# Two start-up loads of a hybrid decoder layer moved from SyncE's queue to ScalarE's

## The chip, the cores and the metric

One core of one Trainium2 chip runs the whole kernel. The metric is the device time of one execution in microseconds. A core has several engines with instruction streams of their own: TensorE (PE in the profile, with its weight loads as PEld), VectorE (DVE), ScalarE (ACT), GpSimd (POOL) and SyncE (SP). A DMA is issued by an instruction on one of them (SPq, ACTq, POOLq in the profile) and is then carried by the core's 16 DMA engines.

## The reference

One layer, float32, 512 tokens of width 1024:

```python
h = rms_norm(x, norm_mix_w)
proj = h @ w_in                       # z, xBC, dt, q, k, v, f
y_ssd = ssd_mixer(xbc, z, dt, ...)    # causal conv, SiLU, chunked scan, gated norm
y_fox = fox_mixer(q, k, v, f, ...)    # causal attention with forget gates
x = x + concat(y_ssd, y_fox) @ w_out
hf = rms_norm(x, norm_ffn_w)
x = x + conv_gated_mlp(hf, w_up, conv_w, conv_b, w_down)
```

## The kernel before

Every large product runs as three TensorE matmuls on split operands: each float32 operand is split into a high part (a rounding copy on ScalarE, names that end in `h`) and a low part (the rest, a subtraction on VectorE, names that end in `l`), and `mm3` (line 91) issues high x high, low x high and high x low. Weights come by `load_split` (lines 79 to 85) through three raw buffers.

The change is in the start-up. x arrives transposed in eight blocks of 128x512 (256 KB each, `load_x`, line 147), each into a buffer of its own. `split_x` turns block k into `xh[:, k]` on ScalarE (line 162) and `xl[:, k]` on VectorE (line 163), both scaled with a column of `mix`, the norm weights, which arrive in one tile with the small dt and forget-gate weights (`load_dt`, 132 KB: load at line 169, ScalarE's rounding at line 171, GpSimd's subtraction at line 172). The first feature tile's weights (tile 8 of xBC) arrive in two halves of 128x512 (256 KB, rows of 2 KB out of rows of 4 KB, `load_first`, line 153) and are split at lines 157 and 158. Half 0 holds the weights of x blocks 0 to 3, half 1 those of blocks 4 to 7. A 128x16 copy (line 113, `warm`) is ScalarE's first instruction, and the load of its activation table stands before it in the trace.

TensorE first multiplies a constant tile in 8 matmuls at line 188 that serve no output. Then for each block k it computes the dt and forget-gate columns (lines 196 and 200) and the first feature tile (`first_product`, line 91, three matmuls). For k = 0 only the dt matmuls run, with filler matmuls on the constant (line 184) between and after them; `first_product(0)` is put behind the dt matmuls of k = 1. The order around the first blocks is fixed in the program. The second feature tile (tile 10) follows on TensorE at once, its weights loaded and split by `load_split`.

All DMAs of the start-up are issued by SyncE, in this order: dt weights, x0, x1, first half of the feature weights, x2, x3, second half, x4 to x7, then constants, further weights and x in token order. An instruction list for each engine is fixed when the program is built, by a scheduler with a timeline of its own; engines run their lists in order. ScalarE's list in the start-up is: table load, warm copy, dt weights, x0, x1, first half, x2, x3, second half, x4 to x7.

Of the kernel before, what the change touches and what calls it, by code (L numbers as in the profile page):

```python
# [38 lines left out]
def tile_hybrid_layer(  # L39
# [20 lines left out]
    nc = tc.nc  # L60
    act, dve, pool, pe = nc.scalar, nc.vector, nc.gpsimd, nc.tensor
# [10 lines left out]
    def raw(ap):  # L72
        return ap.bitcast(F32)
# [36 lines left out]
    mhalf = cp.tile([P, 16], F32, tag="mhalf", name="mhalf")  # L110
    dve.memset(mhalf, -0.5)
    warm = cp.tile([P, 16], F32, tag="warm", name="warm")
    act.copy(warm, mhalf)

    x2 = cp.tile([P, NTB, D], F32, tag="x2", name="x2")

# [27 lines left out]

    def load_x(k):
        xr = px.tile([P, SEQ], F32, tag="xr", name="xr", bufs=NK)
        nc.sync.dma_start(xr, xT[k])
        return xr

    def load_first(half):  # L150
        c = slice(half * 512, (half + 1) * 512)
        w = px.tile([P, 512], F32, tag="wr", name="wr", bufs=2)
        nc.sync.dma_start(w, wxbc[8][:, c])
        return c, w

    def split_first(c, w):
        act.copy(first[0][:, c], w)
        dve.tensor_tensor(out=first[1][:, c], in0=w, in1=raw(first[0][:, c]), op=ALU.subtract)

    def split_x(k, xr):  # L160
        w = mix[:, k : k + 1]
        act.activation(xh[:, k, :], xr, AF.Copy, scale=w)
        dve.scalar_tensor_tensor(
            out=xl[:, k, :], in0=xr, scalar=w, in1=raw(xh[:, k, :]), op0=ALU.mult, op1=ALU.subtract
        )

    def load_dt():
        raw_dt = px.tile([P, NK + NK * 32], F32, tag="wdr", name="wdr")
        nc.sync.dma_start(raw_dt, wdtf)
        w = raw_dt[:, NK:].rearrange("p (k m) -> p k m", m=32)  # L170
        act.copy(wdt[:, :, 0:32], w)
        pool.tensor_tensor(out=wdt[:, :, 32:64], in0=w, in1=raw(wdt[:, :, 0:32]), op=ALU.subtract)
        return raw_dt[:, 0:NK]
# [12 lines left out]

    for _ in range(WARM):
        pe.matmul(spin[:, :P], ones, ones, start=True, stop=True)
    mix = load_dt()
    for k in range(NK):  # L190
        xr = load_x(k)
        split_x(k, xr)
        if k in (1, 3):
            split_first(*load_first(k // 2))
    for k in range(NK):
        ins = pe.matmul(pdt[:64, :], wdt[:, k, :], xh[:, k, :], start=k == 0, stop=False, skip_group_check=True)
        if k < 2:
# [504 lines left out]
    for half in range(2):  # L702
        c = slice(half * 512, (half + 1) * 512)
# [101 lines left out]
    def gated(j):  # L805
        both = []
        for part in range(2):
            f = part * NFF + j
            o = early[part] if j == 0 else up_proj((f,), 1)[0]
            xp = pu.tile([P, SEQ], F32, tag="up", name="up", bufs=3)  # L810
            dve.tensor_mul(xp, o, R2)  # L811
            a = pu.tile([P, SEQ], F32, tag="ua", name="ua", bufs=5)
            cw = C_FCW + 3 * f
            act.activation(a, xp, AF.Identity, scale=pc[:, cw + 2 : cw + 3], bias=pc[:, C_FCB + f : C_FCB + f + 1])
            for s in range(1, 3):
                dve.scalar_tensor_tensor(  # L816
                    out=a[:, s:], in0=xp[:, : SEQ - s], scalar=pc[:, cw + 2 - s : cw + 3 - s], in1=a[:, s:],
                    op0=ALU.mult, op1=ALU.add,
                )
            both.append(a)  # L820
        act.activation(both[0], both[0], AF.Silu)
        return both
# [12 lines left out]
    for j in range(NH):  # L835
# [5 lines left out]
        k, val = gated(j + NH)  # L841
# [178 lines left out]
```

## Time and profile before

| quantity | value |
|---|---|
| median of 3 runs | 799.24 us (798.89 to 799.96) |
| time of the profiled execution | 799.38 us |
| its span, first to last instruction | 797.6 us |
| TensorE busy | 790.3 us (99%) |
| VectorE, ScalarE, GpSimd busy | 567.6, 428.8, 224.4 us |
| mean granted TensorE clock | 0.999 of full speed |

Starts and durations are in us from the start of the span. A wait is attributed to what released it. "DMA to landing" is the time from the issue to the arrival of all data. The rows stand further below.

### The profile page before, as it was taken

What the parts mean: (1) busy time and instruction counts of PE and PEld (TensorE: products, weight loads), DVE (VectorE), ACT (ScalarE), POOL (GpSimd) and SP (SyncE); (2) the same over time, 40 slices, a digit from 0 to 9 for tenths busy, and PEclk for the clock granted to TensorE, in tenths of its full rate; (3) what the DMA queues carried; (4) which work ended last, traced back from release to release, by engine and by line L of the source; (5) the groups of instructions that cost most, each with busy time, mean ns of one, the idle gap of its engine ahead of it and who ended that gap; (6) DMA issues with size and microseconds to landing.
All of it is one profiled execution on the core that took longest, in us unless ns stands there. A gap on an engine that the chain in (4) does not pass through costs nothing.

```text
span 797.6 us, 10600 instructions
## 1 busy us (share of the span) xinstructions
PE 790.3 (99%) x3789; PEld 644.6 (81%) x3789; DVE 567.6 (71%) x889; ACT 428.8 (54%) x779; POOL 224.4 (28%) x260
## 2 busy tenths in 40 slices
PE   9999999999999999999999999999999999999997
PEld 6888878878887877887877888888888888888886
DVE  4896998688567575597874687676676676778754
ACT  7557556542478576776752554344344344556541
POOL 0004322433233352242101333223333223233120
PEclk9999999999999999999999999999999999999999
DMA  9514332341244244252221463323323323399982
GB/s 333 186 66 164 109 106 65 132 132 54 90 155 139 65 119 138 61 172 72 92 88 54 155 163 106 105 82 104 105 82 103 106 81 104 95 250 192 222 181 90
DMA packets 31253, 98.12 MB, mean 123 GB/s; under 512 B 3872, under 2 KB 4960, under 8 KB 31200
## 3 DMA queue, kind: packets, MB, share of 16 engines
q1 hardware_dynamic: 26192, 81.71, 31.0%
q0 software_dynamic: 4576, 15.21, 10.2%
q8 instruction: 30, 0.49, 0.3%
q10 hardware_dynamic: 432, 0.52, 0.2%
q14 instruction: 23, 0.19, 0.1%
HBM read 91.56 MB, written 2.20 MB: 118 GB/s over the span
## 4 chain that ended last, share of the span: by engine, by line
PE 98%; DMA 1%; SPq 0%; DVE 0%; ACT 0%; DVEq 0%; issue 0%
PE up L91 30%; PE pw L91 22%; PE po L91 11%; PE g L91 7%; PE Y L91 6%; PE X L91 4%; PE Z L91 4%; PE o L610 2%; PE pT L600 2%; PE yd L436 2%; PE j L91 1%; PE S L577 1%; PE S L578 1%; PE qkT L527 1%; PE yo L442 1%; PE st L449 1%
## 5 line engine op out<-in xcount | busy, mean ns | idle before, releaser
L84 ACT CAST wh<-wraw 128x1024 fp32r<-128x1024 f32 x103 | 108.0, 1049 | 109.6 <-PE up L91 75.2
L85 DVE TENSOR_TENSOR wl<-wraw,wh 128x1024 fp32r<-128x1024 f32 x103 | 132.8, 1289 | 26.2 <-ACT wh L84 23.9
L91 PE MATMUL up<-hh,wh 128*128 128x512 f32 (+1 forms) x360 | 138.9, 386 | 0.0
L91 PE MATMUL up<-hh,wl 128*128 128x512 f32 (+1 forms) x360 | 138.5, 385 | 0.0
L91 PE MATMUL up<-hl,wh 128*128 128x512 f32 (+1 forms) x360 | 138.5, 385 | 0.0
L91 PE MATMUL pw<-wh,xh 128*128 128x512 f32 x256 | 102.5, 402 | 0.0
L91 PE MATMUL pw<-wl,xh 128*128 128x512 f32 x256 | 101.8, 398 | 0.0
L91 PE MATMUL pw<-wh,xl 128*128 128x512 f32 x256 | 101.2, 397 | 0.0
L91 PEld LDWEIGHTS up<-hh,wh 128*128 128x128 f32 x360 | 67.6, 188 | 13.7 <-issue 0.2
L91 PEld LDWEIGHTS up<-hl,wh 128*128 128x128 f32 x360 | 67.7, 188 | 13.6 <-issue 0.2
L91 PEld LDWEIGHTS up<-hh,wl 128*128 128x128 f32 x360 | 67.6, 188 | 13.3
L811 DVE TENSOR_TENSOR up<-up,R 128x512 f32<-128x512 f32 x44 | 30.3, 691 | 58.5 <-PE up L91 58.5
L816 DVE SCALAR_TENSOR_TENSOR ua<-up,pc,ua 128x511 f32<-128x511 f32 (+1 forms) x88 | 66.8, 763 | 1.3
L91 PEld LDWEIGHTS pw<-wh,xl 128*128 128x128 f32 x256 | 48.2, 188 | 9.9 <-issue 0.5
L91 PEld LDWEIGHTS pw<-wl,xh 128*128 128x128 f32 x256 | 48.2, 188 | 9.6 <-issue 0.7
L91 PEld LDWEIGHTS pw<-wh,xh 128*128 128x128 f32 x256 | 48.1, 188 | 9.5 <-issue 0.7
L765 ACT CAST wh<-T 128x1024 fp32r<-128x1024 f32 (+1 forms) x30 | 29.3, 976 | 36.9 <-PE Z L91 15.3
L579 DVE CUSTOM_DVE_ANT_0 prob<-S,prob 128x128 f32<-128x128 f32 (+1 forms) x64 | 30.3, 487 | 24.7 <-PE S L578 24.4
L766 DVE TENSOR_TENSOR wl<-T,wh 128x1024 fp32r<-128x1024 f32 (+1 forms) x30 | 33.8, 1134 | 19.2 <-ACT wh L765 18.8
L583 ACT ACTIVATE prob<-prob,nm 128x128 f32<-128x128 f32 (+1 forms) x64 | 35.8, 560 | 21.1 <-DVE nm L579 20.4
L258 DVE TENSOR_TENSOR x<-po,x 128x512 f32<-128x512 f32 x48 | 32.6, 685 | 13.1 <-PE po L91 12.9
L826 POOL TENSOR_TENSOR ua<-ua 128x512 f32<-128x512 f32 x11 | 15.0, 1364 | 90.9 <-DVE ua L816 90.9
(231 smaller groups left out, 1690.0 us busy)
## 6 DMA issues: line engine op xcount, KB each, us to landing
wraw<-in_wup_dram SPq DMA_DIRECT2D x44, 512.0 KB, 3.3
T<-in_wdown_dram POOLq DMA_DIRECT2D x20, 512.0 KB, 6.9
wraw<-in_wqk_dram SPq DMA_DIRECT2D x16, 512.0 KB, 3.4
wraw<-in_wout_dram SPq DMA_DIRECT2D x16, 512.0 KB, 3.3
wraw<-in_wxbc_dram SPq DMA_DIRECT2D x11, 512.0 KB, 6.3
wraw<-in_wdown_dram SPq DMA_DIRECT2D x10, 512.0 KB, 3.5
T<-in_wdown_dram SPq DMA_DIRECT2D x10, 512.0 KB, 5.0
wraw<-in_wz_dram SPq DMA_DIRECT2D x8, 512.0 KB, 3.7
```

The costliest lines, as they stand in the source:

```text
L84: act.copy(h, r)
L85: dve.tensor_tensor(out=l, in0=r, in1=raw(h), op=ALU.subtract)
L91: ins = pe.matmul(o, a, b, start=start and n == 0, stop=stop and n == 2, **kw)
L258: dve.tensor_add(dst, banks[tb], dst)
L436: pe.matmul(yd[:, h * HD : (h + 1) * HD], sc[:, h, :], xdt[:, h * HD : (h + 1) * HD], start=True, stop=True)
L579: dve.tensor_tensor_reduce(out=p, in0=sps[:, :n], in1=p, scale=-1.0, scalar=-NEG, op0=ALU.add, op1=ALU.min, accum_out=nm[:, qb : qb + 1],)
L583: act.activation(p, p, AF.Exp, scale=-1.0, bias=nm[:, qb : qb + 1], accum_out=sm[:, qb : qb + 1])
L600: pe.transpose(t[:, w : w + P], prob[:, o : o + P], ident)
L765: act.copy(h[:, :n], src[:, :n])
L766: dve.tensor_tensor(out=l[:, :n], in0=src[:, :n], in1=raw(h[:, :n]), op=ALU.subtract)
L811: dve.tensor_mul(xp, o, R2)
L816: dve.scalar_tensor_tensor(out=a[:, s:], in0=xp[:, : SEQ - s], scalar=pc[:, cw + 2 - s : cw + 3 - s], in1=a[:, s:], op0=ALU.mult, op1=ALU.add,
```

## The change

The loads of x block 1 and of the first half of the feature weights are issued by ScalarE instead of SyncE, on ScalarE's own DMA queue, ahead of the warm copy. SyncE's list keeps the other loads in their old order, so it reads dt weights, x0, x2, x3, second half, x4 to x7. The splits keep their places in the program. No computation changes.

```diff
     warm = cp.tile([P, 16], F32, tag="warm", name="warm")
-    act.copy(warm, mhalf)
...
     def load_x(k):
         xr = px.tile([P, SEQ], F32, tag="xr", name="xr", bufs=NK)
-        nc.sync.dma_start(xr, xT[k])
+        (nc.scalar if k == 1 else nc.sync).dma_start(xr, xT[k])
         return xr
 
     def load_first(half):
         c = slice(half * 512, (half + 1) * 512)
         w = px.tile([P, 512], F32, tag="wr", name="wr", bufs=2)
-        nc.sync.dma_start(w, wxbc[8][:, c])
+        (nc.scalar if half == 0 else nc.sync).dma_start(w, wxbc[8][:, c])
         return c, w
...
     for _ in range(WARM):
         pe.matmul(spin[:, :P], ones, ones, start=True, stop=True)
+    xrs = {1: load_x(1)}
+    firsts = {0: load_first(0)}
+    act.copy(warm, mhalf)
     mix = load_dt()
     for k in range(NK):
-        xr = load_x(k)
-        split_x(k, xr)
+        split_x(k, xrs.pop(k, None) or load_x(k))
         if k in (1, 3):
-            split_first(*load_first(k // 2))
+            split_first(*(firsts.pop(k // 2, None) or load_first(k // 2)))
```

## Rows read from the trace of the kernel before

**Rows 1.** The page, busy time of TensorE over the whole span with its share and its number of matmuls and weight loads.

```profile
PE 790.3 (99%) x3789; PEld 644.6 (81%) x3789; DVE 567.6 (71%) x889; ACT 428.8 (54%) x779; POOL 224.4 (28%) x260
```

**Rows 2.** The view of waits for TensorE's matmuls, all of the span: who waited for whom, us in total, times, longest.

```profile
PE g L188 <- DVE mhalf L111: 1.0, 1, 1.0
PE g L91 <- ACT wh L157: 0.6, 1, 0.6
PE g L196 <- ACT xh L162: 0.3, 1, 0.3
```

**Rows 3.** The chain of work that ended last, in order of time, in the first 30 us: start, duration, what. The one piece that is a transfer.

```profile
2.11 4.64 DMA wr<-in_wxbc_dram
```

**Rows 4.** The timeline of SyncE's DMA issues from 0 to 4 us: start, time on the engine, what (x2 is two issues merged).

```profile
0.73 0.39 SPq L169 DMA_DIRECT2D wdr<-in_wdtf_dram  x1
1.17 0.89 SPq L147 DMA_DIRECT2D xr<-in_xT_dram  x2
2.11 0.43 SPq L153 DMA_DIRECT2D wr<-in_wxbc_dram  x1
2.58 0.91 SPq L147 DMA_DIRECT2D xr<-in_xT_dram  x2
3.53 0.43 SPq L153 DMA_DIRECT2D wr<-in_wxbc_dram  x1
```

**Rows 5.** The view of DMA issues, asked in narrow windows around one issue each: dt weights, x0, x1, first half, x2, second half, in this order. The last column is us from issue to landing.

```profile
wdr<-in_wdtf_dram SPq DMA_DIRECT2D x1, 132.0 KB, 2.2
...
xr<-in_xT_dram SPq DMA_DIRECT2D x1, 256.0 KB, 2.8
...
xr<-in_xT_dram SPq DMA_DIRECT2D x1, 256.0 KB, 3.0
...
wr<-in_wxbc_dram SPq DMA_DIRECT2D x1, 256.0 KB, 4.6
...
xr<-in_xT_dram SPq DMA_DIRECT2D x1, 256.0 KB, 4.9
...
wr<-in_wxbc_dram SPq DMA_DIRECT2D x1, 256.0 KB, 5.3
```

**Rows 6.** Busy time by stretch: stretch, its length, then PE, PEld, DVE, ACT, POOL with instruction counts, granted clock, busy share of the DMA engines, GB/s.

```profile
3.00:4.00 1.00, 1.00 (x7) 1.00 (x7) 0.00 (x0) 0.36 (x2) 0.55 (x1) 1.00 1.03 367
4.00:5.00 1.00, 0.75 (x5) 0.58 (x5) 0.25 (x1) 1.00 (x2) 0.41 (x2) 1.00 0.81 195
5.00:6.00 1.00, 0.88 (x6) 0.66 (x6) 1.00 (x2) 0.38 (x1) 0.00 (x0) 1.00 0.90 223
6.00:7.00 1.00, 0.89 (x6) 0.37 (x5) 0.17 (x1) 0.23 (x1) 0.00 (x0) 1.00 1.01 375
```

**Rows 7.** The timeline of ScalarE from 0 to 9 us: start, duration, what, idle time before it and its releaser.

```profile
0.73 1.28 ACT L113 ACT_TABLE_LOAD   x1 [0.73 <-PEq L1008]
2.02 0.20 ACT L113 COPY warm<-mhalf 128x16 f32<-128x16 f32 x1
2.96 0.41 ACT L171 CAST wdt<-wdr 128x256 fp32r<-128x256 f32 x1 [0.73 <-DMA wdr<-in_wdtf_dram]
4.00 1.38 ACT L162 ACTIVATE xh<-xr,wdr 128x512 fp32r<-128x512 f32 x2 [0.64 <-DMA xr<-in_xT_dram]
6.78 0.62 ACT L157 CAST wh<-wr 128x512 fp32r<-128x512 f32 x1 [1.39 <-DMA wr<-in_wxbc_dram]
7.50 1.38 ACT L162 ACTIVATE xh<-xr,wdr 128x512 fp32r<-128x512 f32 x2
```

**Rows 8.** The timeline of TensorE's matmuls from 4.8 to 16.5 us: the first dt matmul, the last dt matmul of k = 1, the first feature matmul, the first one that needs low weights, the first dt matmul of k = 2, and the first matmul of the second feature tile.

```profile
4.86 0.41 PE L196 MATMUL g<-xh,wdt 128*64 128x512 f32 x1 [0.25 <-ACT xh L162]
...
6.49 0.40 PE L200 MATMUL g<-xl,wdt 128*32 128x512 f32 x1
7.45 0.50 PE L91 MATMUL g<-xh,wh 128*128 128x512 f32 x1 [0.56 <-ACT wh L157]
...
8.17 0.50 PE L91 MATMUL g<-xh,wl 128*128 128x512 f32 x1
...
9.21 0.39 PE L196 MATMUL g<-xh,wdt 128*64 128x512 f32 x1
...
16.19 0.40 PE L91 MATMUL g<-xh,wh 128*128 128x512 f32 x1
```

**Rows 9.** The timeline of VectorE from 4 to 17 us: low parts of x0 and x1, of the first half, of x2 and x3, and of the weights of the second and third feature tile.

```profile
4.75 1.42 DVE L163 SCALAR_TENSOR_TENSOR xl<-xr,wdr,xh 128x512 fp32r<-128x512 f32 x2 [3.74 <-ACT xh L162]
7.43 0.69 DVE L158 TENSOR_TENSOR wl<-wr,wh 128x512 fp32r<-128x512 f32 x1 [1.26 <-ACT wh L157]
8.26 1.42 DVE L163 SCALAR_TENSOR_TENSOR xl<-xr,wdr,xh 128x512 fp32r<-128x512 f32 x2
...
14.28 2.49 DVE L85 TENSOR_TENSOR wl<-wraw,wh 128x1024 fp32r<-128x1024 f32 x2 [1.06 <-ACT wh L84]
```

**Rows 10.** The timeline of GpSimd in the first 25 us, the low part of the dt weights.

```profile
3.45 0.72 POOL L172 TENSOR_TENSOR wdt<-wdr,wdt 128x256 fp32r<-128x256 f32 x1 [2.52 <-ACT wdt L171]
```

**Rows 11.** The timeline from 785 us on: the DMAs that ScalarE issues in this kernel, three merged (start of the first, time from it to the end of the last).

```profile
791.52 2.62 ACTq L918 DMA_DIRECT2D out_dram<-x  x3
```

**Rows 12.** DMA queues from 792 to 793 us, while SyncE's queue (q1) and ScalarE's (q10) both carry outputs: packets, MB, share of the 16 engines' time.

```profile
q10 hardware_dynamic: 103, 0.21, 55.4%
q1 hardware_dynamic: 101, 0.17, 47.6%
```

## The prediction

> **What bounds the kernel now.** I read the page first, then TensorE's waits, then the chain in order of time, and last the timelines of the first 17 us. TensorE is busy 99% of the span [rows 1], and its matmuls wait three times in all, each time in the first 8 us [rows 2]: for the constant of the fillers, for x0's high part (0.3 us) and for the high part of the first half of the feature weights (0.6 us). After that no wait of TensorE is listed, so what it saves or loses at the start should pass through to the end, as long as nothing new comes late. The reader is to see that everything the change can win lies before the matmul at 9.21 us [rows 8].
>
> The chain names the transfer behind the longest wait: the first half of the feature weights, issued at 2.11 and 4.64 us on its way [rows 3], so landed at 6.75. ScalarE splits it at 6.78 after standing idle for 1.39 us [rows 7], and TensorE starts on it at 7.45 [rows 8].
>
> Adding issue time [rows 4] and time to landing [rows 5] gives the order of arrival: dt weights 0.73 + 2.2 = 2.93; x0 1.17 + 2.8 = 3.97; x1 1.64 + 3.0 = 4.64; first half 6.75; x2 2.58 + 4.9 = 7.48; second half 3.53 + 5.3 = 8.83. Between x2 and the second half lies x3, so two blocks take 8.83 - 7.48 = 1.35, or 0.67 us each. x1 took 0.67 after x0 too. The first half took 6.75 - 4.64 = 2.1, which is 1.4 more than its neighbours. In the same stretch the engines move 195 and 223 GB/s at busy shares of 0.81 and 0.90, against 367 before and 375 after [rows 6]. So SyncE isn't late with the issue (it issued the second half before x0 had landed); the transfers are slow from 4 to 6 us, while the DMA engines are nearly all busy. ScalarE's splits after that follow the landings: x2 starts at 7.50, right on its landing at 7.48.
>
> **What a perfect outcome is worth.** If the weights were there in time and x0 were no later, TensorE would run on from the last dt matmul of k = 1 at 6.49 without a gap. Matmuls in the dense stretch are (16.19 - 9.21) / 30 = 0.233 us apart [rows 8], since six blocks of five matmuls lie between these two starts. The six feature matmuls would start at 6.72 and the dt matmul of k = 2 at 6.72 + 6 x 0.233 = 8.12 in place of 9.21: 1.1 us, or 0.14% of the run. That is the ceiling of the mechanism, and 0.2% (1.6 us), about what a measurement here can tell from no change, is above it.
>
> **The change part by part.**
>
> *SyncE loses two issues* of about 0.43 to 0.45 us [rows 4]. x2 and all that follow are issued up to 0.9 us earlier. With over 1 MB already queued in the slow stretch, earlier issue by itself buys nothing; it costs nothing either.
>
> *ScalarE gains two issues ahead of its table load.* The trace has no such issue at the start. ScalarE's own three issues span 2.62 us with waits in them [rows 11], which is the upper bound for the pair; SyncE's 0.43 each is the nearest row of the same size, so I take 0.9 us together. Table load (1.28) and warm copy (0.20) then end at 0.73 + 0.9 + 1.48 = 3.1, where the dt weights were waited for until 2.96 [rows 7]. The split of the dt weights is 0.15 late and ends at about 3.5; GpSimd's part starts at 3.6 and ends by 4.35 [rows 10], before TensorE's first dt matmul at 4.86. ScalarE had been idle 0.64 us before x0, so all this is covered: cost nothing. At the upper bound of 2.62 the split of x0 would start at about 5.2 instead of 4.00, and of these 1.2 us TensorE's gaps before 9.21 (1.1 us, the ceiling) would swallow all but 0.1; the gain would be gone.
>
> *x0 meets company.* x1 and the first half are now issued at 0.73 and about 1.17, beside the dt weights and x0. The first four transfers are the same four (900 KB), only their order differs. Lower end for x0: no change (3.97), if its share isn't touched. Next: x1 goes in ahead of it, one block later, 4.64. Far end: it shares every turn with the first half and lands with it, as late as 6.7. I take 4.64, since the order in which the two queues receive work is dt weights and x1 first, then x0 and the first half. Then the first dt matmul comes 0.67 later (5.5), and TensorE could start on the features at 7.39 rather than 6.72.
>
> *The first half is issued 0.94 earlier* (2.11 - 1.17). At its old 4.64 it would land at 5.8; with x0's 2.8 at 4.0; if its slowness is its own or the DMA engines', at 6.75 as before. I take about 6, nearer to its own row. Its split (0.62) and the low part (0.69 [rows 9]) are then done by 7.4, and the six feature matmuls run at their dense pace from 7.39, so that k = 2 could start at 8.79: a gain of 0.4.
>
> *What is late next.* x2. Its low part ends at 8.26 + 0.71 = 8.97 [rows 9] and is used by the third matmul of k = 2, at 9.21 + 2 x 0.233 = 9.68. If x2 still lands at 7.48, at most some 0.5 to 0.7 us can be gained, whatever the weights do, since the DMA engines pace it. Behind it, the low weights of the second tile end at 14.28 + 1.25 = 15.5 and are needed at 16.19 + 0.47 = 16.66: room for 1.1 us, the ceiling again.
>
> *The sum.* 0 for the issues, - 1.1 for the gaps, + 0.67 for x0, so 0.4 less: 799.38 - 0.4 = 798.98 for the profiled execution's own time. That execution lies 0.14 above the median of the runs, so I forecast 798.9.
>
> **Rivals.**
>
> 1. *The slow stretch goes away* when two queues feed the engines, or x0 isn't delayed: everything from the first half on lands 1.1 to 1.4 earlier, and the whole ceiling is won: 799.24 - 1.1 = 798.1. For it: 195 GB/s is half of what the same engines do a microsecond earlier. Against: they are 0.81 to 0.90 busy [rows 6], so it isn't a lack of queued work.
>
> 2. *The transfers only change places.* The first half is fourth in either order, the engines are the limit, it lands at 6.75 and x2 at 7.48. x0's 0.67 is swallowed by the gap: no change, 799.2. The rows from 792 to 793 us show both queues at work side by side, 55% and 48% of the engines' time, together one full load and no more [rows 12]. The Trainium skill, "DMA: Bandwidth & Descriptors", section "Issuing engines are not separate DMA queues", says this as a rule: DMAs of any issuing engine run on the same 16 engines and interleave, and issuing from several saves only the issue time. By that rule the time is this rival's, and the trace agrees as far as rows 12 go.
>
> 3. *x0 pays (slower).* x0 alternates with the first half and is dragged into its slow stretch. From x0's landing to the first dt matmul take 4.86 - 3.97 = 0.89, from there to the features 1.86 (6.72 - 4.86), from there to k = 2 1.4. k = 2 at 9.21 then means x0 at 5.07: that is the point from which it decides. At 5.3 it costs 0.2, at 6.7 it costs 1.6: 799.4 to 800.9, middle 800.2. For it: x0 is now one of two transfers in flight at a time instead of the next in a line. Against: each block needs only 0.67 us in the fast stretch, and x0 is issued in the same moment as before.
>
> 4. *The change doesn't do what it says.* If the table load stays ScalarE's first instruction (it does not depend on the copy's place by anything that the trace shows), x1 is issued at 2.0 and the first half at 2.5, later than SyncE did at 1.64 and 2.11: 0.35 to 0.4 later, 799.6.
>
> **How the numbers follow.** Forecast (0.4 gained, between 0.1 and 0.7): 0.38. Rival 1: 0.17. Rival 2: 0.22. Rival 3: 0.16. Rival 4: 0.07. The predicted time is the forecast's, 798.9. The range goes from 797.9 (rival 1 and the runs' own spread) to 800.4 (over the middle of rival 3); what lies outside is the bad end of rival 3 and a new order of work that the builder's scheduler may give the engines elsewhere. Faster than 797.6 needs more than the ceiling, or a lucky new order: 0.08. Slower than 800.8 is the far end of rival 3 or an unlucky order: 0.10. The rest, 0.82, is within 0.2%.
>
> **What would show it.** In the new timelines: two ACTq issues at 0.7 and 1.2 ahead of the table load (rival 4 otherwise); x0's split near 4.7 and the first dt matmul near 5.5 (unchanged would be rival 1's side, past 5.95 is rival 3); the first half's split near 6.0, not 6.78 (rival 2); the first feature matmul at about 7.4, and k = 2's first dt matmul at 8.8 instead of 9.21. The stretches from 4 to 6 us should stay near 200 GB/s; if they show 370, it is rival 1. After 10 us TensorE should wait for nothing. The prediction is wrong if a wait of TensorE turns up later, if x2 becomes the wait, or if the difference at 9.21 us doesn't reappear at the end.

## The result and the profile after

| quantity | before | changed |
|---|---|---|
| median of 6 runs | 799.49 us (798.89 to 800.05) | 802.80 us (801.37 to 803.23) |
| profiled execution | 799.38 us | 802.81 us |
| its span | 797.6 us | 801.0 us |

The ratio is 1.0038, 95% interval 1.0028 to 1.0048. The change costs 3.3 us, 0.4%. The forecast was 798.9, a gain, in a range up to 800.4: the time moved the other way and past that range.

TensorE's waits, the view of [rows 2], show what was lost. Columns are us in total, times, longest.

```profile
PE g L197 <- POOL ident masks.py:199: 1.7, 1, 1.7
PE po L91 <- ACT sq L493: 1.4, 1, 1.4
PE g L187 <- DVE mhalf L111: 1.0, 1, 1.0
```

The last one was there before. The other two are the story: the wait ahead of the first dt matmul grew from 0.3 to 1.7 us, and a wait of 1.4 us for ScalarE appears that did not exist. It stands at 178 us, where the prediction said TensorE waits for nothing.

Comparing when TensorE reaches the same matmuls in both traces places the loss: the first dt matmul of k = 2 comes at 11.13 instead of 9.21 (1.9 later); the first tile `j` at 23.6 instead of 21.7 (1.9); the first matmul of `po` at 171.6 instead of 169.8 (1.8); the first score matmul `S` at 224.2 instead of 220.8 (3.4); the first `up` at 448.1 instead of 444.7 (3.4); the span's end 3.4 later. So there are two losses, one before 11 us and one near 178, and nothing is given back.

**The start.** ScalarE's and SyncE's issues, and the splits (the timeline, as in [rows 4] and [rows 7]):

```profile
0.72 0.41 ACTq L146 DMA_DIRECT2D xr<-in_xT_dram  x1
0.73 0.39 SPq L168 DMA_DIRECT2D wdr<-in_wdtf_dram  x1
1.16 0.46 ACTq L152 DMA_DIRECT2D wr<-in_wxbc_dram  x1
1.17 1.37 SPq L146 DMA_DIRECT2D xr<-in_xT_dram  x3
1.65 1.28 ACT L190 ACT_TABLE_LOAD   x1 [1.65 <-PEq L1009]
...
4.54 0.41 ACT L170 CAST wdt<-wdr 128x256 fp32r<-128x256 f32 x1 [1.39 <-DMA wdr<-in_wdtf_dram]
4.85 1.57 ACT L161 ACTIVATE xh<-xr,wdr 128x512 fp32r<-128x512 f32 x2
```

The two new issues stand first, 0.41 and 0.46 us long, and the table load follows. But the dt weights are split at 4.54 instead of 2.96, after ScalarE sat idle for 1.39 us. The last row merges x1 and x0, in this new order: x1's split ended by 5.57, so ScalarE was free when x0 landed at 5.67, and x0's split ended at 4.85 + 1.57 = 6.42; the first dt matmul follows at 6.57. Before, it followed 0.14 after x0's split too, so x0 is what TensorE waited for, although the wait's row names GpSimd's last instruction. The time to landing, the view of [rows 5], of the same narrow windows (dt weights, x1, first half, x0):

```profile
wdr<-in_wdtf_dram SPq DMA_DIRECT2D x1, 132.0 KB, 3.8
xr<-in_xT_dram ACTq DMA_DIRECT2D x1, 256.0 KB, 4.0
wr<-in_wxbc_dram ACTq DMA_DIRECT2D x1, 256.0 KB, 4.8
xr<-in_xT_dram SPq DMA_DIRECT2D x1, 256.0 KB, 4.5
```

Adding issue times: dt weights 0.73 + 3.8 = 4.5 (before 2.93), x1 4.7 (4.64), first half 1.16 + 4.8 = 6.0 (6.75), x0 1.17 + 4.5 = 5.7 (3.97). The two blocks that moved arrive at the same time or earlier; the two that TensorE needs first arrive 1.6 and 1.7 later. The second half, last of the six, lands at 8.0 instead of 8.83: the whole batch is faster, its head is slower. The stretches, in the columns of [rows 6], first one of the kernel before, then the changed one's:

```profile
2.00:3.00 1.00, 1.00 (x7) 1.00 (x6) 0.00 (x0) 0.26 (x3) 0.00 (x0) 1.00 0.92 250
...
2.00:3.00 1.00, 1.00 (x7) 1.00 (x6) 0.00 (x0) 0.99 (x2) 0.00 (x0) 1.00 0.70 74
3.00:4.00 1.00, 1.00 (x7) 1.00 (x7) 0.00 (x0) 0.15 (x1) 0.00 (x0) 1.00 0.90 334
4.00:5.00 1.00, 0.83 (x4) 0.53 (x3) 0.00 (x0) 0.46 (x2) 0.00 (x0) 1.00 1.04 398
5.00:6.00 1.00, 0.00 (x0) 0.00 (x0) 0.40 (x1) 0.86 (x2) 0.97 (x2) 1.00 1.04 373
...
8.00:9.00 1.00, 1.00 (x5) 0.80 (x5) 1.00 (x2) 0.96 (x3) 0.00 (x0) 1.00 1.07 395
```

The slow stretch from 4 to 6 is gone, as rival 1 had it. In its place there is a slow one from 2 to 3: 74 GB/s where the kernel before moved 250. In the stretch from 5 to 6 TensorE has no matmul at all. Its timeline, as in [rows 8]:

```profile
3.77 1.06 PE L187 MATMUL g<-ones 128*128 128x128 f32 x4
6.57 0.66 PE L197 MATMUL g<-xh,wdt 128*64 128x512 f32 x1 [1.74 <-POOL ident masks.py:199]
...
7.77 1.05 PE L183 MATMUL g<-ones 128*128 128x128 f32 x4
...
9.05 0.63 PE L201 MATMUL g<-xl,wdt 128*32 128x512 f32 x1
9.48 0.63 PE L91 MATMUL g<-xh,wh 128*128 128x512 f32 x1
9.90 0.45 PE L91 MATMUL g<-xl,wh 128*128 128x512 f32 x1
10.19 0.40 PE L91 MATMUL g<-xh,wl 128*128 128x512 f32 x1
10.43 0.39 PE L91 MATMUL g<-xh,wh 128*128 128x512 f32 x1
```

The fillers end at 4.83, TensorE idles 1.74 us, and then 512-column matmuls that wait for nothing stand 0.43 us apart (9.05, 9.48, 9.90). From 10.19 on they are 0.24 apart, the dense 0.233 of [rows 8]. So TensorE runs at half its pace for some 3.4 us after the idle time. It did so ahead of it, too: four fillers take 1.06 us before the idle time and 1.05 behind it, where the kernel before needs 0.61 for the later four:

```profile
5.82 0.61 PE L184 MATMUL g<-ones 128*128 128x128 f32 x4
```

Both kernels start at half pace, with fillers 0.21 apart. The kernel before leaves it at 4.2, inside its fillers; the changed one still has it behind its idle time and leaves it at 10.0. The idle time does not slow TensorE down; it goes with a later rise. The granted clock column can't show this: it reads 1.00 wherever the trace holds no clock record, and the first record, for the full clock of 2.4 GHz, begins at 4.2 in the trace of before and at 10.0 in that of the changed kernel, where the pace doubles. The 1.00 of earlier stretches, in [rows 6] too, is no measured clock. The Trainium skill, "TensorE: Matmul & The Clock Gate", section "Back-to-back issue gap", gives a spacing of the columns divided by 1.2 GHz at the lower level, so about 427 ns for 512; the spacing here agrees with it. A record of the lower level itself is in e1, below.

First dt matmul to k = 2 takes 11.13 - 6.57 = 4.56. The prediction's dense sum is 1.86 + 1.4 = 3.26. The half pace costs the difference, 1.3 us. Late x0 by rival 3's own sum (5.67 + 0.89 + 1.86 + 1.4 = 9.82) costs 0.6. Together 1.9, which is the loss at k = 2.

**Near 178 us.** ScalarE, then VectorE and GpSimd, then TensorE, each from its timeline:

```profile
176.09 2.45 ACT L427 ACTIVATE sc<-sc,nacs 128x128 f32<-128x128 f32 x8 [2.24 <-POOL sc L422]
178.45 0.61 ACT L465 ACTIVATE yt<-y 128x512 f32<-128x512 f32 x1
...
179.06 0.67 ACT L493 ACTIVATE sq<-pw,r 128x512 f32<-128x512 f32 x1
```

```profile
173.88 1.23 DVE L85 TENSOR_TENSOR wl<-wraw,wh 128x1024 fp32r<-128x1024 f32 x1 [0.47 <-ACT wh L84]
174.35 1.71 POOL L422 TENSOR_SCALAR_AFFINE_SELECT sc<-sc 128x1024 f32<-128x1024 f32 x1 [9.62 <-DMA sc<-cs_d]
```

```profile
177.97 0.40 PE L91 MATMUL po<-wh,msl 128*128 128x512 f32 x1
179.78 0.50 PE L91 MATMUL po<-wh,msh 128*128 128x512 f32 x1 [1.41 <-ACT sq L493]
```

The 25th matmul of `po`, the first of the third output tile, writes a PSUM bank that a square of the query-key projection (`sq`, line 493) still has to read. That square stands on ScalarE's list behind eight exponentials and another activation. The exponentials wait for GpSimd's select, and this for a DMA (issued at 168.30, 5.90 us) and, as e7 shows, for VectorE's subtraction. The square ends at 179.73, and TensorE starts at 179.78.

Why this is new: the lists that the builder's scheduler fixed for the two kernels differ far beyond the start. Taken in order, the matmuls of the two traces differ in source line or tiles at 291 of 3789 places, all between 13 and 203 us (at none between before and e2, e3 or e10). By the lists, the third `po` tile of before takes a bank released by VectorE and the fourth the one read by the square; after, it is the other way round (the traces show this through the wait alone). The square's bank is needed 12 matmuls, about 2.8 us, earlier. No line of the program around `po` was touched.

### The profile page after: what moved, and what is told of

Its sections match the earlier page's. It is cut to its first block, busy times and chain, and to the rows that moved or that the text cites. A ratio compares the mean times of both kernels' runs of the same rounds, so it can differ in the third digit from the quotient of the medians.

```text
span 801.0 us, 10603 instructions
## 1 busy us (share of the span) xinstructions
PE 791.5 (99%) x3789; PEld 646.0 (81%) x3789; DVE 564.8 (71%) x889; ACT 428.5 (53%) x779; POOL 222.5 (28%) x260
## 3 DMA queue, kind: packets, MB, share of 16 engines
q10 hardware_dynamic: 720, 1.05, 0.4%
## 4 chain that ended last, share of the span: by engine, by line
PE 97%; DMA 1%; ACT 0%; POOL 0%; DVE 0%; issue 0%; DVEq 0%; POOLq 0%
PE up L91 30%; PE pw L91 22%; PE po L91 11%; PE g L91 7%; PE Y L91 6%; PE X L91 4%; PE Z L91 4%; PE o L611 2%; PE pT L601 2%; PE yd L437 2%; PE j L91 1%; PE S L578 1%; PE S L579 1%; PE qkT L528 1%; DMA sc<-cs_d 1%; PE yo L443 1%
```

## The experiments

Theory: two queues at the start delay the dt weights and x0, the idle time this causes keeps TensorE at half pace for longer, and separately the new lists let `po` wait for the square. Rivals: the late wait is only the late start passed on; the half pace is contention or an artefact; the loss at the start comes from ScalarE's list (issues, table load), not from the transfers. Single executions are compared at k = 2 and by their waits; the runs of before beside them have medians from 799.4 to 799.7.

**Square ahead (e1).** The changed kernel, with this edit on the square:

```diff
-            act.activation(sq, o, AF.Square, scale=r[:, tb : tb + 1])
+            with tc.high_priority(AHEAD): act.activation(sq, o, AF.Square, scale=r[:, tb : tb + 1])
```

> The changed kernel with one edit: the square of the query-key block (it alone holds the PSUM bank for which TensorE waits 1.4 us near 180 us) gets a higher priority, which moves it ahead of the last of eight exponentials and of one square on ScalarE's list; all other lists stay word for word. If the late stall is the order of ScalarE's list (with the bank that the third output tile was given), that wait falls by 0.8 to 1.0 us (0.30 for one exponential, 0.6 for the square), to about 0.5, and the span to about 800.1. If the stall follows from the late start alone, it stays at 1.4 and the span at 801.0. The start-up is the same in both: dt matmul of k = 2 near 11.1.

802.63 us (800.29 to 803.04), ratio 1.0029 (1.0016 to 1.0043). The edit missed: TensorE's list is that of the changed kernel, and the square that `po` waits for still stands behind the exponentials (at 179.10). The wait is still 1.4, so this says nothing on the bank. But its trace holds what that of the changed kernel lacks, a record of the lower clock:

```profile
8.00:9.00 1.00, 1.00 (x4) 0.67 (x3) 1.00 (x3) 0.95 (x2) 0.00 (x0) 0.50 1.01 379
```

The clock rose at 4.1 here, ahead of 1.68 us of idle time; the first matmuls behind it ran at full pace. From 7.5 to 10.9 the column reads 0.50, the 1.2 GHz level, and 512-column matmuls stand 0.43 apart. So the spacing of 0.43 is the lower clock, and here it is a fall that came 1.3 us after TensorE was back at work.

**Only the dt weights on ScalarE (e2).** The kernel before, with:

```diff
-        nc.sync.dma_start(raw_dt, wdtf)
+        nc.scalar.dma_start(raw_dt, wdtf); act.copy(warm, mhalf)
```

(and the old warm copy taken out).

> The kernel before, with one load moved: ScalarE issues the dt weights as its first instruction, SyncE issues x0, x1, first half and so on in the old order. TensorE's list is that of before. Sharing theory (each transfer that is needed first loses by what is in flight beside it): x0 is issued 0.44 earlier but shares with the dt weights; x0 lands between 3.5 and 4.0, dt weights between 2.9 and 3.5, k = 2 at 8.8 to 9.3, span 797.2 to 797.7, no difference or up to 0.4 gained. If a second queue by itself makes the first transfers slow, dt weights land after 4 and k = 2 comes past 10, with TensorE at half rate: span 799.5.

800.58 us, 798.5 to 801.58 over 11 runs, ratio 1.0008 (0.9999 to 1.0017). TensorE's list is that of before, and the profiled execution (798.5) has no late wait. Even one transfer on the second queue shifts landings: dt weights at 4.02 (issued 0.01 earlier than in before, landed 1.1 later), x0 at 3.8. The first dt matmul starts at 5.31 after 0.48 idle, at full pace, and k = 2 at 8.48, 0.73 before [rows 8]. So the gain that the prediction looked for exists in one execution; the median of 11 is not better. The runs fall into two groups, five from 798.5 to 799.6 and six from 800.6 to 801.6; what the slower group loses was not seen.

**The new order on one queue (e3).** x1 and the first half first, dt weights and x0 behind them, all by SyncE:

```diff
-    mix = load_dt()
+    xrs = {1: load_x(1)}; firsts = {0: load_first(0)}; act.copy(warm, mhalf); mix = load_dt()
```

> The program text of the change with both loads issued by SyncE: x1, first half, dt weights, x0, x2 and on, all on one queue. TensorE's list is that of before. If what costs is the order (x1 and the half ahead of the dt weights and x0), the dt weights land about 1.4 to 2.8 later than before (4.3 to 5.7), x0 after them, and k = 2 comes at 11 to 12 with TensorE at half rate for some us: span about 799.5 to 800.5. If what costs is the second queue, k = 2 stays below 10 and the span near 798.

802.9 us, one execution. In one queue the order of issue is the order of landing: x1 3.2, first half 3.9, dt weights 5.1. The first half isn't slow by itself, as [rows 3] might suggest: here it lands 0.7 us behind x1. Whether its place or its moment made it slow in the kernel before stays open. TensorE idles 2.1 us, then runs at half pace, and k = 2 starts at 12.42, later than in the changed kernel. TensorE's list is that of before, and there is no late wait. So a late start alone doesn't make that wait.

**Fillers over the idle time (e4).** The changed kernel with more fillers ahead of the first product.

```diff
-WARM = 8
+WARM = 16
```

> The changed kernel with 16 instead of 8 matmuls on the constant ahead of the first dt matmul (the scheduler also lays out other lists anew, so only the start-up is read). If TensorE's half rate from 6.6 to 9.9 comes from its standing idle from 4.8 to 6.6, the bridge keeps it at 0.23 us a matmul, and from the first dt matmul to that of k = 2 it takes 3.3 us as in the ideal (9.8 if it starts at 6.6). If the half rate has another cause, it takes 4.6 us as in the changed kernel. If the fillers themselves run at half rate to their end, they end near 8.3, and k = 2 comes near 11.6.

803.33 us, one execution. No wait for x0 is left: fillers bridge to the first dt matmul at 7.49, and from it to k = 2 (10.52) takes 3.03 us in place of 4.56, at 0.23 per matmul. With the idle time bridged the pace rises at 7.0, inside the fillers, not at 10.0. The transfers still run beside the full pace (402 to 406 GB/s from 6 to 9), so the half pace isn't contention. Without any idle time it lasted to 7.0 here, to 4.2 and 5.2 in the two traces of before: the moment of the rise varies by more than the idle time explains. The later lists changed again (`S` comes 4.9 us after that of before), so the end says nothing.

**Two buffers for the square (e5).** The changed kernel with

```diff
-            sq = pa.tile([P, 512], F32, tag="sq", name="sq", bufs=1)
+            sq = pa.tile([P, 512], F32, tag="sq", name="sq", bufs=2)
```

> The changed kernel with a second buffer for the square of the query-key block. The start-up is that of the changed kernel, and the third output tile still gets the PSUM bank that this square reads; but on ScalarE's list the square now stands ahead of the eight exponentials and of the other square (lists after that place differ too). If the late stall is this bank with this place on ScalarE's list, the wait of 1.4 us of TensorE near 180 us is gone (below 0.2), and the span comes to 799.0 to 800.2. If the stall is the late start's doing, it stays near 1.4 and the span near 801.

By its list the third `po` tile still takes the bank of the square, but ScalarE's list now has the square ahead of the exponentials:

```profile
174.52 0.70 ACT L492 ACTIVATE sq<-pw,r 128x512 f32<-128x512 f32 x1
175.09 1.06 ACT L84 CAST wh<-wraw 128x1024 fp32r<-128x1024 f32 x1
176.74 2.46 ACT L426 ACTIVATE sc<-sc,nacs 128x128 f32<-128x128 f32 x8 [0.58 <-POOL sc L421]
```

The 25th matmul of `po` follows the 24th at once (179.71, 179.94): with the square's place moved, the wait goes. The time isn't what was expected: 806.33 us (804.85 to 807.97, the slowest being the profiled one), ratio 1.0082 (1.0065 to 1.0098). The dt weights landed at 4.92 and x0 at 6.2, worse than in the changed kernel with the same issues (k = 2 at 12.51), and the new lists lose some 5 us more behind `po` (`up` starts 8.9 us after that of before, `po` 3.5). Where these 5 us go I have not followed.

**Only x1 on ScalarE (e6); only the first half (e7).** Each has one of the change's two moves alone:

```diff
-        nc.sync.dma_start(xr, xT[k])
+        (nc.scalar if k == 1 else nc.sync).dma_start(xr, xT[k])
```

```diff
-        nc.sync.dma_start(w, wxbc[8][:, c])
+        (nc.scalar if half == 0 else nc.sync).dma_start(w, wxbc[8][:, c])
```

TensorE's list is that of the changed kernel in both.

> Only x1 is issued by ScalarE, the first half stays with SyncE behind x0. All lists but the first rows of ScalarE's and SyncE's are those of the changed kernel. Sharing theory: x1 (256 KB) alone pushes the dt weights and x0 back, dt weights at 3.5 to 4.5, x0 at 4.6 to 5.3; first dt matmul 5.5 to 6.2, and TensorE at half rate after it if it stood idle over a microsecond. The late wait of 1.4 us stays, since the list is the same. If only the pair of transfers does harm, the dt weights land at 3 and x0 at 4, and k = 2 comes near 9.2.

> Only the first half is issued by ScalarE, x1 stays with SyncE behind x0. Sharing theory: the half (256 KB) beside the dt weights and x0 pushes them back as x1 does, dt weights 3.5 to 4.5, x0 4.6 to 5.3; in addition ScalarE's list has the half's split ahead of x0's, so x0's split waits for 0.6 more where the half lands late. First dt matmul 5.6 to 6.6. If the harm comes from x1 alone, first dt matmul near 4.9 and k = 2 near 8.2 to 8.8. The late wait of 1.4 us stays, since TensorE's list is that of the changed kernel.

e6: 802.37 us, k = 2 at 10.59 (1.4 late), half pace, late wait 1.4. e7: 800.81 us, k = 2 at 10.72 (1.5 late), half pace, but no late wait, against what I expected. Either move alone costs most of the start's loss. The late wait's absence in e7 shows how it is made; ScalarE and TensorE there:

```profile
174.30 2.46 ACT L426 ACTIVATE sc<-sc,nacs 128x128 f32<-128x128 f32 x8 [0.65 <-POOL sc L421]
...
177.28 0.66 ACT L492 ACTIVATE sq<-pw,r 128x512 f32<-128x512 f32 x1
```

```profile
177.77 0.40 PE L91 MATMUL po<-wh,msl 128*128 128x512 f32 x1
178.01 0.48 PE L91 MATMUL po<-wh,msh 128*128 128x512 f32 x1
```

The scores' DMA took 4.9 us instead of 5.9 and GpSimd's select 1.09 instead of 1.71, so the square ended at 177.94, just as the bank was needed at 178.0. The new list leaves no slack there. What decides is in VectorE's and GpSimd's rows of e7:

```profile
173.68 1.66 DVE L85 TENSOR_TENSOR wl<-wraw,wh 128x1024 fp32r<-128x1024 f32 x1 [0.46 <-ACT wh L84]
173.17 1.09 POOL L421 TENSOR_SCALAR_AFFINE_SELECT sc<-sc 128x1024 f32<-128x1024 f32 x1 [8.64 <-DMA sc<-cs_d]
```

The DMA landed early enough for the select to start ahead of VectorE's subtraction. The select took 1.09 us, and the subtraction 1.66 instead of 1.23, ending 1.08 behind it; e9 is the same (1.09, 1.93, 1.07). In the changed kernel, e1, e6, e8 and e12 the subtraction started first, and the select, 1.64 to 2.04 us long, ended 0.94 or 0.95 behind it each time. The times of these seven traces fit two instructions that run one after the other, and the wait was 1.4 or none by which came first: 0.47 us decided in the changed kernel, 0.51 in e7.

**Two tiny loads on ScalarE (e8).** The kernel before, with two loads of 1.5 KB and 8 KB, which SyncE issues later otherwise, issued first by ScalarE:

```diff
-    mix = load_dt()
+    v = cp.tile([P, 3], F32, tag="v", name="v"); nc.scalar.dma_start(v, pdtf); nc.scalar.dma_start(dsk, ssd_d[0:1, :].to_broadcast([P, SSD_HEADS])); act.copy(warm, mhalf); mix = load_dt()
```

> The kernel before with two small loads (1.5 KB and 8 KB) issued by ScalarE as its first instructions, the large ones all on SyncE in the old order. It has the two issues ahead of the table load and a second queue, but no bytes to speak of. Sharing theory: dt weights near 2.9 to 3.1, x0 near 4.0 to 4.2, first dt matmul at 4.9 to 5.1, k = 2 at 9.2 to 9.4. If it is the issues ahead of the table load or a second queue as such that does the harm, dt weights or their split come after 3.9, and the first dt matmul after 5.5. Later lists differ, so only the start-up is read.

802.54 us, one execution. ScalarE's list carries the same two issues and the late table load, and the dt weights land at 2.83 and are split at 3.05: neither the issues nor the table load cost anything at the start, which settles that rival. But x0, expected unharmed, lands at 5.3:

```profile
3.00:4.00 1.00, 1.00 (x7) 1.00 (x7) 0.32 (x2) 0.56 (x3) 0.46 (x1) 1.00 0.80 107
4.00:5.00 1.00, 0.83 (x4) 0.53 (x3) 0.00 (x0) 0.00 (x0) 0.50 (x2) 1.00 0.41 93
```

Against 367 and 195 of [rows 6]. So here it is not the bytes of the second queue that delay the first. These loads are made of many short rows (the second one of 128 rows of 64 B, 4.4 us to landing), which the change's are not; how far the shortness does it stays open. The late wait of 1.4 for the square is there as well, with a list of matmuls that is neither that of before nor that of the changed kernel.

**The issues a little later (e9).** The changed kernel, with the warm copy, and so the table load, put ahead of the two issues.

```diff
+    tc.keep_in_program_order(act.copy(warm, mhalf))
     xrs = {1: load_x(1)}
     firsts = {0: load_first(0)}
-    act.copy(warm, mhalf)
```

(both issues stand in `tc.keep_in_program_order` as well).

> The changed kernel with ScalarE's two issues behind its table load and warm copy instead of ahead of them, so at about 2.2 and 2.7 us. If the dt weights and x0 are late because other transfers run beside them from the first moment, they land at 2.9 and 4.0 to 4.4 here, the first dt matmul comes at 4.9 to 5.3 at full rate, and k = 2 at 9.0 to 9.8 (the first half is the last of the first five to be issued). If a second queue does harm whenever it is used in the start-up, the first dt matmul comes past 5.6. TensorE's list is that of the changed kernel, so the late wait may appear: between 0 and 1.4.

800.55 us, one execution. The issues came at 1.05 and 1.51, during the table load (0.72 to 2.00), so only 0.33 and 0.35 later. That is enough to bring the dt weights to 3.23 (0.3 later than before), and from 2 to 3 us the engines moved 244 GB/s. x1 lands at 3.85 and is split at 3.88, as the first of the two in this list. x0 lands at 1.17 + 3.5 = 4.67, 0.7 later than before:

```profile
4.65 0.72 ACT L162 ACTIVATE xh<-xr,wdr 128x512 fp32r<-128x512 f32 x1
```

The first dt matmul follows at 5.52, after 0.69 idle, still at half pace; k = 2 at 10.09 (0.9 late). The prediction had x0 one block late at 4.64 and the first dt matmul at 5.5: that is this trace, in which the rate did not fall. TensorE's list is that of the changed kernel; no late wait.

**Before once more (e10); before with fewer fillers (e11).** The first has no edit; the second:

```diff
-WARM = 8
+WARM = 4
```

> The kernel before, unchanged, for a second profile of its start-up. If one queue makes the start steady, the dt weights land at 2.8 to 3.1, x0 at 3.9 to 4.2, and k = 2 comes at 9.0 to 9.5. If the start-up scatters from execution to execution here as well (the changed start-up has put the dt weights between 3.9 and 4.9), dt weights or x0 differ by over 0.5 from 2.93 and 3.97, and single traces can't carry differences of that size.

> The kernel before with 4 instead of 8 matmuls on the constant: TensorE stands idle from about 2.8 to 4.9, while no transfer is touched (later lists differ; only the start-up is read). If the idle time costs TensorE its rate, the four dt matmuls and their fillers, from the first dt matmul to the last of k = 1, take 2.5 to 2.9 us as in the changed kernel, not the 1.63 of before, and the matmuls stand 0.43 apart. If the half rate came from something else in the changed start-up, they take 1.6 as before.

e10: 799.44 us, dt weights at 2.9, x0 at 4.27, k = 2 at 9.28; the one-queue start repeats within 0.3 in its landings and 0.1 at k = 2. e11: 801.82 us. Transfers are undisturbed (x0 at 3.87), only TensorE idles:

```profile
4.76 0.66 PE L196 MATMUL g<-xh,wdt 128*64 128x512 f32 x1 [1.64 <-ACT xh L162]
...
7.24 0.63 PE L200 MATMUL g<-xl,wdt 128*32 128x512 f32 x1
7.67 0.78 PE L91 MATMUL g<-xh,wh 128*128 128x512 f32 x1
8.25 0.63 PE L91 MATMUL g<-xl,wh 128*128 128x512 f32 x1
8.68 0.63 PE L91 MATMUL g<-xh,wl 128*128 128x512 f32 x1
```

x0 is used 0.1 earlier than in [rows 8], but from the first dt matmul to the last of k = 1 takes 2.48 in place of 1.63, and k = 2 starts at 10.38, 1.17 late, just as the pace rises. With fewer fillers it rose 5 to 6 us later than in the two traces of before, with more of them (e4) 3 us earlier than in the changed kernel: that is the evidence that idle time at the start puts off the rise, on one trace each. (The span is 2.4 us longer, not 1.2; the later lists differ, and two waits of 0.4 and 0.3 us are new.)

**A version that might win (e12).** e2 with two more fillers.

```diff
-WARM = 8
+WARM = 10
```

> The dt weights on ScalarE's queue, as in the run of that name, and 10 matmuls on the constant to bridge to the first dt matmul. If its slow executions (over 800.5) are those in which TensorE stood idle too long before the first dt matmul, they become rarer, and the start-up stays at k = 2 near 8.5 to 9.3. But the list gives the third output tile the bank of the late square again: if that costs 1.4, the median is 800 to 800.6; if it doesn't strike, 798.5 to 799.0, faster than before.

800.75 us (799.66 to 801.7, 10 runs), ratio 1.0015 (1.0006 to 1.0025). k = 2 starts at 8.91, 0.3 early, but the two added fillers changed the later lists too, and the wait of 1.4 for the square is there. No version beat the kernel before.

## Why the prediction was wrong

- **What bounds the kernel, and the ceiling.** Right as far as the start goes: what is lost before 9.21 reappears in full at `j` and `po`. A gain of 1.1 was the most to win; the loss had no such bound, and the range treated it as if it had.
- **Issues and table load at no cost.** Right. 0.41 + 0.46 = 0.87 against 0.9 taken, and e8 shows the dt weights split at 3.05 behind the same two issues. Rival 4 is refuted: the table load stands behind the issues.
- **The failed step: "x0 meets company".** The dt weights were taken as untouched and x0 as one block later, 4.64. Measured: 4.5 and 5.7, with the first dt matmul at 6.57, past the sign of 5.95 that was set for rival 3. Choosing 4.64 rested on turn-taking by blocks at the old rate, and the rate itself fell, from 250 to 74 GB/s between 2 and 3 us. Where it didn't (e9, 244 GB/s), x0 landed at 4.67: by that trace 0.7 of x0's 1.7 us is the block ahead of it, and the 1.0 that the prediction left out came with the fall. Rival 3 had the direction, the place and the deciding point (x0 at 5.07) right; its sum at the measured landing is 0.6. Four executions with the change's issues (the changed kernel, e1, e4, e5) had the dt weights at 4.5, 3.9, 3.9 and 4.9 and x0 at 5.7, 5.3, 5.4 and 6.2, with 74, 179, 202 and 100 GB/s from 2 to 3 us, against 250, 229 and 234 in three with all issues on SyncE in the old order (before, e10, e11). All four are past the point, and they vary far more than before did. In e2, e6, e7 and e12, with one load on ScalarE's queue, the rate was 86 to 196, in e3, one queue in the new order, 356.
- **A term that the sum did not have: the half pace,** 1.3 us. The prediction counted every matmul behind a late x0 at 0.233. [Rows 8] start at 4.86, behind the rise at 4.2, and show idle times of 0.25 and 0.56 alone; the half pace stood in the filler rows ahead of them, which the prediction does not show.
- **The first half at about 6.** Right (5.96), and rival 1's side came with it: no slow stretch from 4 to 6. It bought nothing, because with x0 late and half pace TensorE didn't reach the weights before 9.48.
- **Rival 2 and its rule.** The Trainium skill, "DMA: Bandwidth & Descriptors", section "Issuing engines are not separate DMA queues", has it that DMAs of several issuers share the same engines and interleave. The traces agree that nothing was won by a second issuer. The order of landing is a part of what hurt: x1 now lands ahead of x0 (4.7 and 5.67). That the rate of all together falls for the first microsecond is not in that sentence.
- **"After 10 us TensorE should wait for nothing".** Wrong, by 1.41 us. "A new order of work that the builder's scheduler may give the engines elsewhere" was named and left outside the range without a price. It had one to find: the bank that `po` takes, and what stands ahead of its reader on ScalarE. e3 (late start, TensorE's list of before, no wait) and e5 (square moved, no wait) show that the list makes the wait; e7 and e9 show that it makes it possible, not certain: with the changed kernel's list three traces have it and two do not, by whether GpSimd's select starts ahead of VectorE's subtraction.

The sum that would have been right: + 0.6 for x0, + 1.3 for the half pace, + 1.4 for the bank, 3.3 us; the two profiled executions differ by 3.43.

**Open:** why two queues lower the rate from 2 to 3 us, and why an issue 0.33 us later (e9) brings the rate back; what sets the moment at which TensorE's pace rises; what the slower runs of e2 lose. Delaying the second queue's issues beyond 1.05 us was not tried.

## What to carry to other kernels

Leave the transfers that the first product needs alone in flight: a second queue that starts beside them can bring the batch home earlier and still make its head later, and the head is what counts. Whenever a change can lengthen an idle time of TensorE near the start, price what comes behind it at half pace too, and check the spacing of equal matmuls rather than a clock column that reads 1.00 where nothing was recorded. Where a scheduler lays out the lists, a start-up edit is also an edit of everything behind it: compare the lists, and look for buffers that changed hands with little slack.

## What was not expected of the hardware

- All traces start at half pace. It ended at 4.2 to 5.2 us where TensorE's idle time ahead of the first dt matmul was 0.21 to 0.48 us (before, e2, e10, e12), at 7.0 with none (e4), and at 9.0 to 12.7 where it was 0.69 to 2.23 (the changed kernel, e3, e5 to e9, e11). In e1 it ended at 4.1, and behind 1.68 us of idle time it came back, from 7.5 to 10.9. No limit is read from this.
- ScalarE issued two DMAs at 1.05 and 1.51 while its table load ran from 0.72 to 2.00 (e9): the load did not hold up the issues.
- Loads of 9.5 KB in all on a second queue brought the engines to about 100 GB/s for 2 us (e8), with their busy share still at 0.80 in the first of them.
- GpSimd's select and VectorE's subtraction near 174 us did not run side by side: whichever started second ended 0.94 to 1.08 us behind the other, and its time grew from 1.09 to as much as 2.04 or from 1.23 to as much as 1.93 (seven traces, under e7).
